# The first gate and up blocks of two FFNs: seven products in place of two whole blocks, in an order of their own

## The chip, the cores and the metric

The kernel runs on one core of a Trainium2 chip. The metric is the device time of one execution in microseconds (us), as the median of several runs. One execution was also recorded by the hardware profiler; all times of instructions are from that record. The engines are TensorE (PE), VectorE (DVE), ScalarE (ACT), GpSimd (POOL) and SyncE (SP), each with a queue of its own that it works off in order; DMAs are issued from SP and POOL.

## The reference, cut to what matters

Two layers over 512 tokens of width 1024: latent attention with an FFN, then chunked attention with an FFN. The change lies in both FFNs:

```python
def rms_norm(x, g):
    xf = x.astype(jnp.float32)
    y = xf * lax.rsqrt(jnp.mean(xf * xf, axis=-1, keepdims=True) + EPS)
    return (y * g.astype(jnp.float32)).astype(x.dtype)

def swiglu(h, w_gate, w_up, w_down):
    return (jax.nn.silu(h @ w_gate) * (h @ w_up)) @ w_down
```

Here h is the normed x (512 x 1024), and w_gate and w_up are 1024 x 2816, which is 22 column blocks of 128. All is float32.

## The kernel before, in words

Each float32 operand is split into two parts of the PE's fp32r type: ACT casts the value (`whi`, `th`, `xh`), DVE subtracts the cast from the value (`wlo`, `tl`, `xl`). One product of 128 rows of weights is then three matmuls (high by high, high by low, low by high). A weight tile of 1024 columns so costs one cast of ACT (L144) and one difference of DVE (L145); its data come by DMA into `raw`.

The FFN works on x before its norm's factor is known. Gate and up of blocks 0 and 1 are computed in four PSUM banks, the tokens in two halves, since the first half of x is ready earlier (`half`). Blocks 2 and 3 are computed next, whole, 96 matmuls of 128x512 in all (`proj`). In the meantime the sum of squares is transposed (`tot`), the factor is computed (`rstd`) and spread over partitions (`bc`), and the blocks are gated: gate times factor, silu, times up.

The 18 other blocks run as nine pairs. A pair's two blocks times the two halves of the width and the two halves of the tokens make a 2 x 2 by 2 x 2 block product, done by seven products instead of eight (`products`): 168 matmuls of 128x256 per pair, 24 per product. Weight sums (`sums`, `plus`) feed four of the seven; sums of blocks of x (`blocks_of`: the tiles `xg`, `t1`, `t3`, split into `th` and `tl`) are the moving operands. Products 1, 3, 4 and 5 accumulate in one pair of PSUM banks (`al`), product 2 has its own (`ga`), and products 0 and 6 share a third (`be`). Since each stands as a running sum that several results need, ACT or DVE take a copy out of a bank in between: of `be` after product 0 (`ut`), of `al` after products 1, 3 and 5 (`gt`, `gt`, `ut`). After product 6 the pair is gated.

The first pair's weight sums were made by DVE, from tiles that SP loads; from the second pair on, two of the sums come by DMAs on POOL's queue that add to what lies in the tile (`begin`), and DVE makes the two others. Down then runs over the gated blocks.

The order on each engine is set by a scheduler from the order of the code and priorities; `issue_after` (in the code also `behind`) makes one instruction stand after another. Weight tiles are split two ahead of the product that uses them (`feed.next(1024, 2)`).

## Time and profile before

| | |
|---|---|
| runs | 1103.98, 1104.80, 1104.91 us; median 1104.8 |
| profiled execution | 1105.07 us; its span, first to last instruction, 1103.3 us |
| mean granted PE clock | 0.997 |
| PE busy | 1092.4 us, 99% of the span, 6893 matmuls |
| DVE busy | 908.5 us, 82% |
| ACT busy | 678.3 us, 61% |
| POOL busy | 117.1 us, 11% |
| layer 0: blocks 2 and 3 / first pair begin | 212.07 us / 234.8 us |
| layer 1: the same | 787.20 us / 809.9 us |

Times within the span count from its first instruction. A row of the timeline has start, duration, engine, line, operation and the names of output and inputs, then in brackets the idle time ahead of it and what ended that. A duration runs until the result is there; where two instructions follow at once, the second starts a little before the first one's duration is over, so the cost of one in a queue is the difference of the starts. A line of the waits has the waiting engine and tile, the releasing engine and tile, then the sum, count and longest in us. The chain of waits names, for each stretch of time, the instruction that what comes later depended on.

### The profile page before, as it was taken

The page shows a single profiled execution, that of the slowest core. Times are in us where ns is not written, and L with a number is a line of the kernel's source. Part 1 is how long each engine was busy: PE and PEld are TensorE (multiplying, and loading weights), DVE is VectorE, ACT ScalarE, POOL GpSimd, SP SyncE. Part 2 cuts the span into 40 slices and gives each one's busy share as a digit, 9 for nine tenths or more (in the row PEclk, how much of TensorE's full clock was granted, in tenths as well). Part 3 has the DMA queues.
Part 4 walks back from the last instruction along what each step waited for, and adds up shares of the span by engine and source line. Part 5 has one row for each costly group of instructions (what it writes and reads, how often), then busy time and mean ns, then how long its engine had stood idle before and what let it go on. Part 6 is the DMA issues. An engine that isn't in the chain of part 4 may idle for free.

```text
span 1103.3 us, 19079 instructions
## 1 busy us (share of the span) xinstructions
PE 1092.4 (99%) x6893; PEld 978.8 (89%) x6893; DVE 908.5 (82%) x1659; ACT 678.3 (61%) x1323; POOL 117.1 (11%) x181
## 2 busy tenths in 40 slices
PE   9999999999999999999999999999999999999997
PEld 6887889999999998888888888889899999998885
DVE  7787747988878889978858898758988889789977
ACT  7575737655555556668636767657645555556675
POOL 2211100101000001500000110000100010001401
PEclk9999999999999999999999999999999999999999
DMA  7344226447787757961555677634638888758913
GB/s 240 120 116 142 62 68 238 143 116 184 171 202 184 180 167 248 164 191 49 190 153 156 173 192 186 168 121 161 198 103 214 228 207 223 216 178 249 171 29 76
DMA packets 88334, 181.47 MB, mean 164 GB/s; under 512 B 26816, under 2 KB 28608, under 8 KB 88240
## 3 DMA queue, kind: packets, MB, share of 16 engines
q1 hardware_dynamic: 74752, 147.10, 43.1%
q0 software_dynamic: 13056, 32.73, 16.4%
q8 instruction: 54, 0.88, 0.3%
q10 hardware_dynamic: 432, 0.44, 0.1%
q14 instruction: 40, 0.33, 0.1%
HBM read 148.88 MB, written 10.88 MB: 145 GB/s over the span
## 4 chain that ended last, share of the span: by engine, by line
PE 97%; DVE 1%; ACT 1%; issue 1%; DMA 0%; POOL 0%; DVEq 0%; POOLq 0%; SPq 0%; ACTq 0%
PE al L1550 19%; PE b L377 11%; PE b L378 11%; PE b L379 11%; PE be L1550 9%; PE al L1306 8%; PE be L1306 5%; PE ga L1550 5%; PE de L1306 3%; PE ga L1306 3%; PE pt L561 2%; PE b L1707 2%; PE b L1107 1%; PE sc L1699 1%; PE sc L1698 1%
## 5 line engine op out<-in xcount | busy, mean ns | idle before, releaser
L144 ACT CAST whi<-raw 128x1024 fp32r<-128x1024 f32 (+3 forms) x220 | 221.0, 1006 | 205.6 <-PE al L1550 71.5
L145 DVE TENSOR_TENSOR wlo<-raw,whi 128x1024 fp32r<-128x1024 f32 (+3 forms) x220 | 255.8, 1164 | 67.1 <-ACT whi L144 66.1
L1550 PE MATMUL al<-th,whi 128*128 128x256 f32 x432 | 122.8, 284 | 0.0
L1550 PE MATMUL al<-th,wlo 128*128 128x256 f32 x432 | 121.0, 280 | 0.0
L1550 PE MATMUL al<-tl,whi 128*128 128x256 f32 x432 | 121.0, 280 | 0.0
L377 PE MATMUL b<-xh,whi 128*128 128x512 f32 x234 | 96.7, 415 | 0.0
L378 PE MATMUL b<-xl,whi 128*128 128x512 f32 x234 | 91.8, 392 | 0.0
L379 PE MATMUL b<-xh,wlo 128*128 128x512 f32 x234 | 91.7, 392 | 0.0
L1550 PEld LDWEIGHTS al<-th,whi 128*128 128x128 f32 x432 | 81.3, 188 | 2.2
L1550 PEld LDWEIGHTS al<-th,wlo 128*128 128x128 f32 x432 | 81.3, 188 | 0.2 <-DVE wlo L145 0.2
L1550 PEld LDWEIGHTS al<-tl,whi 128*128 128x128 f32 x432 | 81.3, 188 | 0.0
L548 ACT ACTIVATE p<-p,mn 128x128 f32<-128x128 f32 (+1 forms) x96 | 54.1, 563 | 36.0 <-DVE mn L546 34.1
L145 DVE TENSOR_TENSOR ptl<-pt,pth 128x128 fp32r<-128x128 f32 (+1 forms) x96 | 46.6, 485 | 30.5 <-ACT pth L144 29.6
L145 DVE TENSOR_TENSOR wlo<-wd,whi 128x512 fp32r<-128x512 f32 x86 | 56.3, 684 | 14.6 <-ACT whi L144 14.4
L144 ACT CAST whi<-wd 128x512 fp32r<-128x512 f32 x86 | 49.8, 618 | 25.0 <-PE al L1306 10.7
L144 ACT CAST pth<-pt 128x128 fp32r<-128x128 f32 (+1 forms) x96 | 40.3, 422 | 32.2 <-PE pt L561 31.3
L171 POOL DMA_DIRECT2D raw<-in_w_pair x32 | 28.1, 895 | 285.9 <-DVE ut L1562 84.1
L379 PEld LDWEIGHTS b<-xh,wlo 128*128 128x128 f32 x234 | 43.9, 188 | 9.9 <-DVE wlo L145 0.3
L1306 PE MATMUL al<-whi,pl 128*128 128x512 f32 x132 | 51.5, 390 | 0.0
L1306 PE MATMUL al<-wlo,ph 128*128 128x512 f32 x132 | 51.4, 389 | 0.0
L1306 PE MATMUL al<-whi,ph 128*128 128x512 f32 x132 | 51.4, 389 | 0.0
L377 PEld LDWEIGHTS b<-xh,whi 128*128 128x128 f32 x234 | 44.2, 189 | 5.7 <-ACT whi L144 0.2
(320 smaller groups left out, 3391.2 us busy)
## 6 DMA issues: line engine op xcount, KB each, us to landing
raw<-in_w_pair SPq DMA_DIRECT2D x88, 512.0 KB, 4.6
raw<-in_w_pair POOLq DMA_DIRECT2D x32, 512.0 KB, 7.6
wd<-in_w_down SPq DMA_DIRECT2D x54, 256.0 KB, 6.0
raw<-in_w_o SPq DMA_DIRECT2D x16, 512.0 KB, 4.0
raw<-in_w_gu SPq DMA_DIRECT2D x16, 512.0 KB, 4.7
raw<-in_w_down SPq DMA_DIRECT2D x16, 512.0 KB, 4.3
raw<-in_w_qkb SPq DMA_DIRECT2D x16, 512.0 KB, 3.5
wd<-in_w_down POOLq DMA_DIRECT2D x22, 256.0 KB, 5.0
```

The source lines that it names most:

```text
L144: return (nc.scalar.copy(dst_hi, src), V.tensor_tensor(dst_lo, src, dst_hi.bitcast(F32), op=OP.subtract))
L145: V.tensor_tensor(dst_lo, src, dst_hi.bitcast(F32), op=OP.subtract))
L171: nc.gpsimd.dma_start(r[j], self.src[n], accum_op=OP.add)
L377: nc.tensor.matmul(o, l[0], r[0], start=start, stop=False)
L378: nc.tensor.matmul(o, l[0], r[1], start=False, stop=False)
L379: last_mm[0] = nc.tensor.matmul(o, l[1], r[0], start=False, stop=stop)
L548: nc.scalar.activation(p[:, :n], p[:, :n], AF.Exp, bias=mn[:, :1], scale=-1.0, accum_out=self.sums[:, qt:qt + 1])
L561: nc.tensor.transpose(t[:, kt * P:(kt + 1) * P], p[:, kt * P:(kt + 1) * P], ident)
L1107: nc.tensor.matmul(o[:, q_], va[kt][:, part, v_], pt[:, kt, q_], start=n + kt == 0, stop=n == 2 and kt == NQT - 1)
L1306: nc.tensor.matmul(to[e], l[c], r[d], start=j < 4 and k == 0 and n == 0, stop=k == NF // 2 - 1 and n == 2, skip_group_check=True)
L1550: nc.tensor.matmul(o, l[c], r[d], start=first_ and n == 0, stop=k == K2 - 1 and n == 2, skip_group_check=True)
L1707: nc.tensor.matmul(o[:, q_], vv, pt[:, kt, q_], start=pt is pth and kt == 0, stop=pt is ptl and kt == NQT - 1)
```

## The change

Blocks 2 and 3 leave the whole form (`N_WHOLE` from 4 to 2) and become a first pair, so that ten pairs run in place of nine. For that pair alone:

- Its seven products run in the order 1, 2, 0, 3, 6, 4, 5 (`FIRST_TURN`), and each product's matmuls are bound to stand after the one before.
- Its four weight sums come by DMAs on POOL's queue that add to a tile in SBUF: r0 is chunk 2 plus chunk 3, r3 is chunk 0 plus r0, r6 is chunk 1 plus r3, and r4 is chunk 2 plus chunk 0. The third waits for the second and the second for the first (`chain`); DVE makes none of them.
- The sums of blocks of x begin ahead of the second half of blocks 0 and 1; their later parts are laid between the differences of the weights of products 6, 4 and 5 (`step`).
- The fetch of x moves behind certain weight loads on SP's queue (`get_x`).
- ACT copies the four PSUM banks of blocks 0 and 1 to SBUF (`fu`). Squares, norm factor and its spreading move into the second and third pair, and the gating of blocks 0 and 1 and of the pairs becomes a list of units (`units`), taken one at a time within later pairs.
- In layer 1, a side job (`by_tokens`) starts in the third pair in place of the second.

The diff, cut to its core ("..." where lines are left out):

```diff
--- before.py
+++ after.py
-N_WHOLE = 4
+N_WHOLE = 2
...
+    FIRST_TURN = (1, 2, 0, 3, 6, 4, 5)
...
         def begin(self):
-            r, self.made = self.raw, True
-            r[0] = r[3] = r[6] = self.tile(2, wide[0], "sum", 2)
+            r = self.raw
+            r[0] = self.tile(2, wide[0], "sum", 2)
+            if self.turn[0]:
+                r[3] = self.tile(0, wide[0], "sum", 2)
+                r[6] = self.tile(1, wide[0], "sum2", 2)
+            else:
+                r[3] = r[6] = r[0]
             r[4] = self.tile(2, wide[0], "sum2", 2)
-            for j, n in ((0, 3), (4, 0)):
-                with tc.issue_after(last_pow[0].ins):
-                    nc.gpsimd.dma_start(r[j], self.src[n], accum_op=OP.add)
+            self.add(0, self.src[3])
+            self.add(4, self.src[0])
+
+        def add(self, j, src):
+            with tc.issue_after(last_pow[0].ins):
+                nc.gpsimd.dma_start(self.raw[j], src, accum_op=OP.add)
+
+        def chain(self):
+
+            self.add(3, self.raw[0])
+            self.add(6, self.raw[3])
...
         def sums(self, j):
...
-            if j == 0 and not self.made:
-                r[0] = r[3] = r[6] = wide[0].tile([P, 1024], F32, tag="sum", name=name_("raw"), bufs=2)
-                plus(r[0], r[4], r[5])
-            elif j in (3, 6):
+            if j in (3, 6) and not self.turn[0]:
                 plus(r[j], r[j], r[j // 3])
-            elif j == 4 and not self.made:
-                plus(r[4], r[4], r[1])
-            elif j == 1 and self.then:
+            if j == (3 if self.turn[0] else 1) and self.then:
                 self.then.begin()
...
-                for j in range(7):
-                    self.plan.append((pair, 1024, j, None))
+                if not p:
+                    pair.turn = FIRST_TURN
+                for j in pair.turn:
+                    self.plan.append((pair, 1024, j, None if p or j != 3 else "h"))
...
+            if not h:
+                with behind(feed.loaded):
+                    next(p for p, *_ in feed.plan[feed.pos:] if isinstance(p, Pair)).begin()
...
                 feed.ahead(2 if late else 3)
+                feed.loaded = get_x(feed.loads[feed.pos + (4 if late else 5)])
...
-        x = fetch(x_src)
+        x = []
         post = Post(G_APOST[i], H)
-        last = out_proj(osp, KT, post, firsts, 2, late)
+        last = out_proj(osp, KT, post, firsts, 2, late, lambda after: fetch(x_src, x, after))
...
-        sx.squares(0)
-        post.apply(x, 1, sx.each)
+        base = feed.pos
+        pair = feed.plan[base][0]
+        pair.chain()
+        feed.behind[base + 2] = feed.behind[base + 3] = post.apply(x, 1, sx.each)
+        tb, hid = [], Hidden(H)
+        more = blocks_of(x, G_FPRE[i], H, tb)
+        next(more)
+        feed.ahead(3)
         run(half(1))
-        sx.squares(1)
         for k in range(KT):
             nc.sync.dma_start(a["mid"][:, k], x[k])
-        tb = []
-        more = blocks_of(x, G_FPRE[i], H, tb)
-        next(more)
-        b = [bank(), bank()]
-        rest = proj(2, KT, 4, xs, b)
-        some(rest, 3)
-        v = sx.sum.total()
-        r = rstd(v)
+        kept = [H(name="fu") for _ in banks]
+        for t, b in zip(kept[:2], banks[:2]):
+            nc.scalar.copy(t, b)
+        with behind(next(more)[0]):
+            for t, b in zip(kept[2:], banks[2:]):
+                empty = nc.scalar.copy(t, b)
         eps = sp.tile([P, 4], F32, tag="eps", name=f"eps_{i}", bufs=1)
-        V.tensor_scalar(eps, v, EPS, None, op0=OP.mult)
-        some(rest, 7)
-        rb = spread_sb(r)
-        next(more)
-        banks.extend(b)
-        hid = Hidden(H)
-
-
-        for f in range(N_WHOLE):
-            if f < 3:
-                b = banks[2 * f:2 * f + 2]
-                if f == 2:
-                    run(rest)
-            else:
-                b = [bank(), bank()]
-                run(proj(2, KT, 4, xs, b))
-            t = U(name="gt")
-            V.tensor_tensor(t, b[0], rb, op=OP.mult)
+        rb = []
+
+        def norm():
+            v = sx.sum.total(None, 300)
+            with first(300):
+                r = rstd(v)
+            V.tensor_scalar(eps, v, EPS, None, op0=OP.mult)
+            rb.append(r)
+
+        def spread_():
+            rb[0] = spread_sb(rb[0])
+
+        def gate(t, u):
+            V.tensor_tensor(t, t, rb[0], op=OP.mult)
             nc.scalar.activation(t, t, AF.Silu)
             h = hid.room()
-            V.scalar_tensor_tensor(h, t, -1.0, b[1], op0=OP.mult, op1=OP.mult)
+            V.scalar_tensor_tensor(h, t, -1.0, u, op0=OP.mult, op1=OP.mult)
             hid.add(h)
-            if f == 1:
-                next(more)
-        products(xs, tb, rb, hid, by_tokens(H) if i else None)
+
+        low = []
+
+        def step(n):
+            low[:] = next(more)[1:] if not low else low
+            feed.lows[base + n] = low[0]
+            feed.split(base + n)
+            with behind(feed.low):
+                low[:] = next(more)[1:]
+            feed.lows[base + 6] = low[0]
+
+        side = {(0, 2): lambda: step(4), (0, 0): lambda: step(5), (1, 1): lambda: sx.squares(0),
+                (1, 4): lambda: sx.squares(1), (1, 6): norm, (2, 2): spread_}
+        units = [lambda f=f: gate(*kept[2 * f:2 * f + 2]) for f in range(N_WHOLE)]
+        products(xs, tb, rb, hid, side, units, empty, low, by_tokens(H) if i else None)
...
-        yield
+            last = split(*cut(out[k][0], A1), m[:, A1])
+        yield last
         for k in K2:
             u, v, m, n = ts[k]
             V.tensor_tensor(n[:, A0], v[:, A1], u[:, A1], op=OP.subtract)
             V.scalar_tensor_tensor(n[:, A1], m[:, A1], -1.0, v[:, A0], op0=OP.mult, op1=OP.subtract)
-            split(*out[k][1], n)
-        yield
+            last = split(*out[k][1], n)
+            if k:
+                yield last
...
-    def products(xs, tb, rb, hid, aside=None):
+    def products(xs, tb, rb, hid, side, units, empty, low, aside=None):
...
+        def gated(t, u):
+            V.tensor_tensor(t, t, rb[0], op=OP.mult)
+            nc.scalar.activation(t, t, AF.Silu)
+            h = hid.room()
+            V.tensor_tensor(h, t, u, op=OP.mult)
+            hid.add(h)
+
         pairs = (NF - N_WHOLE) // 2
+        done = mm = None
         for p in range(pairs):
             al, ga = [], []
             be = [bank("t" if p % 2 else "s", "be") for _ in range(2)]
-            gate = [U(name="gt") for _ in range(2)]
-            up_ = [U(name="ut") for _ in range(2)]
-            for j in range(7):
-                if aside is not None and p and j in (0, 1, 3, 5):
+            make = U if p > 3 else hid.make
+            gate = [make(name="gt") for _ in range(2)]
+            up_ = [make(name="ut") for _ in range(2)]
+            for j in (range(7) if p else FIRST_TURN):
+                if (p, j) in side:
+                    side[p, j]()
+                if p > 1 and j in ((3, 5) if p == 2 else (1, 3, 5)) and units:
+                    units.pop(0)()
+                if aside is not None and p > 1 and j in (0, 2, 4, 5, 6):
                     next(aside, None)
                 w = feed.next(1024, 2)
+                done = None if p else mm
                 if p + 1 == pairs and j >= 4:
                     hid.ahead(j // 5)
                 if j == 1:
@@ -1546,16 +1587,22 @@
                     for k in range(K2):
                         l, r = w(e * S + k * P, P), moving[j][k]
                         first_ = j < 3 and k == 0
-                        for n, (c, d) in enumerate(((0, 0), (0, 1), (1, 0))):
-                            nc.tensor.matmul(o, l[c], r[d], start=first_ and n == 0, stop=k == K2 - 1 and n == 2,
-                                             skip_group_check=True)
+                        with behind(done):
+                            for n, (c, d) in enumerate(((0, 0), (0, 1), (1, 0))):
+                                mm = nc.tensor.matmul(o, l[c], r[d], start=first_ and n == 0, stop=k == K2 - 1 and n == 2,
+                                                      skip_group_check=True)
                     t, u = gate[e], up_[e]
                     if j == 0:
                         nc.scalar.copy(u[:, A1], o)
+                        if not p:
+                            with behind(low[0]):
+                                V.tensor_tensor(t[:, A0], t[:, A0], ga[e][:, A0], op=OP.add)
                     elif j == 1:
-                        nc.scalar.copy(t[:, A0], o)
+                        with behind(None if p else empty):
+                            nc.scalar.copy(t[:, A0], o)
                     elif j == 2:
-                        V.tensor_tensor(t[:, A0], t[:, A0], o, op=OP.add)
+                        if p:
+                            V.tensor_tensor(t[:, A0], t[:, A0], o, op=OP.add)
                     elif j == 3:
                         nc.scalar.copy(t[:, A1], o)
                     elif j == 4:
@@ -1564,11 +1611,10 @@
                         nc.scalar.copy(u[:, A0], o)
                     else:
                         V.tensor_tensor(t[:, A1], t[:, A1], o, op=OP.add)
-                        V.tensor_tensor(t, t, rb, op=OP.mult)
-                        nc.scalar.activation(t, t, AF.Silu)
-                        h = hid.room()
-                        V.tensor_tensor(h, t, u, op=OP.mult)
-                        hid.add(h)
+                        units.append(lambda t=t, u=u: gated(t, u))
+                        while p > 6 and units:
+                            units.pop(0)()
```

How this moves instructions. On ACT, around the copies of product 0 in the first pair. Before (`be_635` is product 0's bank, `gt_618`, `gt_624`, `gt_633` belong to the gating of whole blocks, `th_585` is the last sum of x):

```order
L144 CAST th_581_2616<-t3_598_2641 128x512
L144 CAST th_585_2620<-t3_602_2649 128x512
L144 CAST whi_645_2874<-raw_611_2697 128x1024
L1200 ACTIVATE gt_624_2784<-gt_624_2784 128x512
L1554 COPY ut_639_2862<-be_635_2858 128x256
L1200 ACTIVATE gt_633_2849<-gt_633_2849 128x512
L144 CAST whi_648_2907<-raw_630_2819 128x1024
L1554 COPY ut_640_2863<-be_636_2859 128x256
L1556 COPY gt_637_2860<-al_650_2911 128x256
```

After (`be_604` and `be_605` are the banks of products 0 and 6, `al_610` and `al_611` those of 1, 3, 4 and 5; `whi_618` holds the weights of product 4, `whi_620` those of product 5, `whi_622` those of the next pair; `gt_606` L1602 copies product 1, L1607 product 3):

```order
L1198 COPY fu_602_2641<-b_530_2259 128x512
L1198 COPY fu_603_2642<-b_531_2260 128x512
L1602 COPY gt_606_2666<-al_610_2670 128x256
L1602 COPY gt_607_2667<-al_611_2671 128x256
L144 CAST whi_618_2744<-raw_522_2171 128x1024
L144 CAST th_559_2465<-t3_576_2482 128x512
L144 CAST th_563_2469<-t3_580_2490 128x512
L144 CAST whi_620_2806<-raw_492_2083 128x1024
L1607 COPY gt_606_2666<-al_610_2670 128x256
L144 CAST th_567_2473<-t3_584_2498 128x512
L1607 COPY gt_607_2667<-al_611_2671 128x256
L144 CAST th_571_2477<-t3_588_2506 128x512
L1596 COPY ut_608_2668<-be_604_2664 128x256
```

Before, the copy of product 0 stood ahead of product 1's copies; now it stands behind those of products 1 and 3 and behind the last four casts of the sums of x.

On DVE, the sums of x and the weight differences that those casts alternate with, after the change (`raw_521` is r6, so `wlo_614` belongs to product 6; `raw_522` is r4):

```order
L146 TENSOR_TENSOR tl_560_2466<-t3_576_2482,th_559_2465 128x512
L146 TENSOR_TENSOR tl_564_2470<-t3_580_2490,th_563_2469 128x512
L146 TENSOR_TENSOR wlo_614_2709<-raw_521_2169,whi_613_2708 128x1024
L1364 TENSOR_TENSOR t3_584_2498<-xg_582_2496,xg_581_2495 128x256
L1365 SCALAR_TENSOR_TENSOR t3_584_2498<-t1_583_2497,xg_582_2496 128x256
L146 TENSOR_TENSOR tl_568_2474<-t3_584_2498,th_567_2473 128x512
L146 TENSOR_TENSOR wlo_619_2745<-raw_522_2171,whi_618_2744 128x1024
L1364 TENSOR_TENSOR t3_588_2506<-xg_586_2504,xg_585_2503 128x256
L1365 SCALAR_TENSOR_TENSOR t3_588_2506<-t1_587_2505,xg_586_2504 128x256
```

Before, these sums and their differences stood between the splits of whole blocks, behind the squares and ahead of the gating; now each waits in turn for a cast on ACT and has a weight difference between it and the next.

On POOL, the DMAs of the first pair's weight sums (layer 0, after the change):

```order
L182 DMA raw_519_2165<-in_w_pair 128x1024
L496 TENSOR_TENSOR r_552_2349<-ss_551_2347,mhalf_92 128x2
L182 DMA raw_520_2167<-raw_519_2165 128x1024
L182 DMA raw_522_2171<-in_w_pair 128x1024
L182 DMA raw_521_2169<-raw_520_2167 128x1024
L182 DMA raw_594_2521<-in_w_pair 128x1024
```

The four DMAs on `raw_519` to `raw_522` are new; `r_552`, a factor of the norm behind attention, and the last DMA, which begins the next pair's sums, were there before.

More of the change, by code (lines that the diff above doesn't have):

```diff
@@ L140, in first, with split @@
         tc.cur_priority += n
-    def split(dst_hi, dst_lo, src):
-        return (nc.scalar.copy(dst_hi, src),
-                V.tensor_tensor(dst_lo, src, dst_hi.bitcast(F32), op=OP.subtract))
+    def split(dst_hi, dst_lo, src, after=None):
+        hi = nc.scalar.copy(dst_hi, src)
+        with behind(after):
+            return hi, V.tensor_tensor(dst_lo, src, dst_hi.bitcast(F32), op=OP.subtract)
     def split_scaled(dst_hi, dst_lo, src, col):
@@ L296, in load @@
                 if isinstance(src, Pair):
-                    src.load(j)
+                    self.loads[len(self.raw)] = src.load(j)
                     self.raw.append(None)
@@ L676, in apply, with fetch, out_proj @@
                         (nc.gpsimd if k in (0, 2, 4) else V).tensor_tensor(to(k), x[k][:, c], t, op=self.op)
-                    each(k, h)
-    def fetch(src, make=U):
-        x = []
-        for k in range(KT):
-            t = make(name="x")
-            nc.sync.dma_start(t, src[:, k])
-            x.append(t)
-        return x
-    def out_proj(rhs, n_k, post, have, n_last, late):
+                    at = each(k, h)
+            return at
+    def fetch(src, x, after=None):
+        with behind(after):
+            for k in range(KT):
+                t = U(name="x")
+                ins = nc.sync.dma_start(t, src[:, k])
+                x.append(t)
+        return ins
+    def out_proj(rhs, n_k, post, have, n_last, late, get_x):
         done = list(have)
@@ L1319, in blocks_of @@
         for k in range(KT // 2):
-            out.append([(U(F32R, "th"), U(F32R, "tl")) for _ in range(2)])
+            out.append([tuple(m(F32R, n) for n in ("th", "tl")) for m in (U, make if k == 3 else U)])
         K2 = range(KT // 2)
```

21 lines of the change are left out of this document (8 added, 13 removed).

## The prediction

> **What bounds the kernel now.** I read the page's busy times first, then TensorE's waits, then the chain of waits.
>
> ```profile
> PE 1092.4 (99%) x6893; PEld 978.8 (89%) x6893; DVE 908.5 (82%) x1659; ACT 678.3 (61%) x1323; POOL 117.1 (11%) x181
> PE 97%; DVE 1%; ACT 1%; issue 1%; DMA 0%; POOL 0%; DVEq 0%; POOLq 0%; SPq 0%; ACTq 0%
> PE sc L1094 <- ACT kh L144: 1.9, 1, 1.9
> PE warm L113 <- DVE idle L110: 1.2, 1, 1.2
> PE b L377 <- ACT xh L148: 0.2, 1, 0.2
> ```
>
> TensorE (PE) works 1092.4 of 1103.3 us and waits three times in all: 1.9 us in the first attention, 1.2 us at the start, 0.2 us in the second FFN. The chain is 97% PE. Time is thus gained by taking matmuls away and lost by making PE wait; what DVE or ACT do matters only where PE stands behind them. The next view is busy time by stretch. In each layer the first stretch runs from block 2's first matmul to the first pair's, the second over the first pair as far as its sixth product.
>
> ```profile
> 212.07:234.82 22.75, 22.75 (x107) 18.80 (x106) 20.60 (x43) 13.74 (x23) 2.90 (x3) 1.00 0.39 93
> 234.82:254.69 19.87, 19.87 (x169) 19.74 (x168) 16.52 (x24) 10.99 (x17) 0.86 (x1) 1.00 0.58 159
> 787.20:809.92 22.72, 22.72 (x106) 18.80 (x105) 20.09 (x43) 13.78 (x24) 3.22 (x3) 1.00 0.31 70
> 809.92:829.80 19.88, 19.88 (x168) 19.71 (x167) 17.67 (x24) 11.15 (x17) 0.83 (x1) 1.00 0.50 148
> ```
>
> After the window and its length stand PE, PEld, DVE, ACT, POOL (busy us, count), the clock granted to PE, the DMA share and GB/s. PE is full in all four, DVE is at 83% to 91%: beside PE there is little room on DVE.
>
> **The change part by part.** *Two blocks become a pair.* The chain gives the pieces.
>
> ```profile
> 214.30 0.44 PE tot L473 x4
> 219.55 0.44 PE bc L501 x4
> 237.80 2.82 PE al L1550 x24
> 257.70 2.82 PE al L1550 x24
> ```
>
> The two blocks take 22.75 us, in which 0.44 + 0.44 are transposes of the norm that stay. From one pair's second product to the next pair's is 257.70 - 237.80 = 19.90 us, seven products of 2.82 us. So a layer saves 22.75 - 0.88 - 19.90 = 1.97 us of PE, and both layers **3.9 us**, if PE gets through the new pair without waiting.
>
> *It does not, by the order.* The new pair's products run 1, 2, 0, 3, 6, 4, 5. Products 0 and 6 use the same two PSUM banks (`be`), so ACT must copy product 0 out (L1596, `ut_608`) before product 6 begins. Before, products 1 to 5 lay between them, 14.1 us; now only product 3 does, 2.82 us. In ACT's order that copy stands behind `gt_607`, which reads the second half of product 3 itself, and behind the cast `th_571`. `th_571` needs `t3_588`, which stands on DVE behind two 1024-column weight differences and two 512-column ones. For durations I use rows of the same operations in the trace of before (start to start where the next follows at once).
>
> ```profile
> 207.04 1.32 ACT L1325 ACTIVATE xg<-x,gains 128x512 f32<-128x512 f32 x2
> 217.17 1.00 ACT L144 CAST th<-t 128x256 fp32r<-128x256 f32 x3
> 220.02 0.59 ACT L508 COPY bc<-bc 128x512 f32<-128x512 f32 x1
> 229.39 1.05 ACT L144 CAST whi<-raw 128x1024 fp32r<-128x1024 f32 x1 [0.79 <-PE b L378]
> 230.35 1.66 ACT L144 CAST th<-t 128x512 fp32r<-128x512 f32 x3
> 236.43 0.37 ACT L1554 COPY ut<-be 128x256 f32<-128x256 f32 x1
> 236.69 0.64 ACT L1200 ACTIVATE gt<-gt 128x512 f32<-128x512 f32 x1
> 229.81 0.41 DVE L1338 TENSOR_TENSOR t<-xg,xg 128x256 f32<-128x256 f32 x1
> 230.15 0.41 DVE L1339 SCALAR_TENSOR_TENSOR t<-t,xg 128x256 f32<-128x256 f32 x1
> 230.99 0.69 DVE L145 TENSOR_TENSOR tl<-t,th 128x512 fp32r<-128x512 f32 x1 [0.44 <-ACT th L144]
> 231.60 1.22 DVE L145 TENSOR_TENSOR wlo<-raw,whi 128x1024 fp32r<-128x1024 f32 x1
> 232.74 0.68 DVE L145 TENSOR_TENSOR tl<-t,th 128x512 fp32r<-128x512 f32 x1
> ```
>
> ACT: 0.96 for a 1024-column cast (229.39 to 230.35), 0.52 to 0.55 for a 512-column one (1.66 for three), 0.30 for a 256-column one (1.00 for three, less the tail of the last), 0.62 for `xg` (1.32 for two), 0.48 for a 512-column copy (0.59 less its tail), 0.27 for a 256-column copy (236.43 to 236.69). DVE: 0.34 for 256 columns, 0.60 for 512, 1.14 for 1024 (231.60 to 232.74).
>
> I wrote the two orders out with these durations, each instruction starting when its engine is free and its inputs are done, from the same point of layer 0 as the trace (197 us). With the order of before this puts the start of Down within 0.5 us of the trace. With the new one: product 1 starts on PE at 212.0 (22.75 us of blocks no longer ahead of it), 2 at 214.8, 0 at 217.7, 3 at 220.5, and 6 is due at 223.4. ACT is at `fu_600` at 211.5 and has 8.1 us of work without a gap: two `fu` copies, four `xg`, four 256-column casts, `whi_613`, two `fu`, two `gt` copies, `whi_618` (0.96 + 2.5 + 1.2 + 0.96 + 0.96 + 0.54 + 0.96). So `th_559` starts at 219.5 and is done at 220.2. Then DVE: `tl_560`, `tl_564`, `wlo_614` and `t3_584` (0.60 + 0.60 + 1.14 + 0.75) until 223.3; ACT casts `th_567` until 223.9; DVE `tl_568`, `wlo_619` and `t3_588` (0.60 + 1.14 + 0.76) until 226.45; ACT casts `th_571` to 227.0 and copies `ut_608` to 227.36. Product 6 starts at 227.4: **PE stands 4.0 us**. Layer 1 has the same rows in the same order, and the ledger gives 4.0 again: **8.0 us** for both.
>
> The ends of this term: from below, `gt_607` cannot start before product 3 ends (223.4 + 0.2 for the last matmul to drain), and `gt_607`, `th_571`, `ut_608` (0.27 + 0.52 + 0.37) follow in one queue, so at least 1.4 us per layer even if DVE were never late. From above, 5 us, if each of the four hand-overs between ACT and DVE takes 0.2 us more. I take 4.0, since only a DVE 2.6 us ahead of the ledger would bring the lower end, and DVE is at 83% to 91% of its time here. Behind `ut_608` on ACT stand `ut_609` and `whi_622`, the next pair's first weights; these wait for the buffer that product 6 gives back, so they move with PE and cost nothing more. On DVE the additions of product 6's banks move with it too.
>
> *What the wait does to PE's clock.* The one long wait of PE in before is followed by this:
>
> ```profile
> 106.67 0.50 PE L1094 MATMUL sc<-kh,qh 128*128 128x128 f32 x2 [1.92 <-ACT kh L144]
> 100.00:104.00 4.00, 4.00 (x22) 3.23 (x21) 3.42 (x10) 3.44 (x10) 0.00 (x0) 1.00 0.47 109
> 104.00:108.00 4.00, 2.08 (x13) 1.57 (x11) 3.38 (x6) 3.60 (x7) 1.28 (x2) 0.94 0.61 152
> 108.00:112.00 4.00, 4.00 (x20) 3.90 (x19) 3.24 (x9) 1.72 (x5) 0.52 (x1) 0.63 0.67 253
> ```
>
> After 1.92 us without matmuls the granted clock falls: 4 x (0.06 + 0.37) = 1.72 us of PE work lost. A stall of 4.0 us is twice as long, and I expect the same after each. Some of the slow stretch can fall inside the stall, where it costs nothing; I take 1.45 of 1.72, with 0.75 and 1.72 as ends, so **2.9 us** for both layers. Waits under 1 us I do not charge with it. [...]
>
> *Other waits.* The gatings of blocks 0 and 1 and of the first two pairs are put off into later pairs, where DVE has 2.2 us of room (17.67 of 19.88).
>
> ```profile
> L1567 DVE TENSOR_TENSOR gt<-gt,bc 128x512 f32<-128x512 f32 x36 | 24.9, 692 | 1.2
> L1570 DVE TENSOR_TENSOR hd<-gt,ut 128x512 f32<-128x512 f32 x36 | 23.1, 683 | 0.0
> ```
>
> One gating more per pair is 0.69 + 0.68 plus about one 256-column sum (0.42), so about 1.8 us, and the room is nearly used up. The ledger finds PE behind DVE or ACT by 0.05 to 0.47 us at two further places in layer 0 (0.4 us in all) and six in layer 1 (1.1): **1.5 us**; ends 0 and 3. The 0.2 us wait of before at `xh` in layer 1 goes, as a third weight difference (1.14) no longer stands ahead of the values it needs on DVE: **-0.2**; next behind it is `xh` of the following tile, 0.6 us early.
>
> *Work that I cost at nothing.* The first pair's sums leave DVE for DMAs that accumulate, each waiting for the one before.
>
> ```profile
> raw<-in_w_pair SPq DMA_DIRECT2D x88, 512.0 KB, 4.6
> raw<-in_w_pair POOLq DMA_DIRECT2D x32, 512.0 KB, 7.6
> ```
>
> With the first base loaded at 186, three links of 7.6 us land at 194, 202 and 209; the last, r6, is read by `whi_613` at 215.8, so 6 us to spare; r4 lands in between. Should the links take 10 us each, the last would come at 216 and begin to push `whi_613`. The x loads go behind weight loads on SP; in the ledger the first is issued near 177 and needed at 184, and the weight loads, larger ones, take 4.6 us. The four `fu` copies (0.48 each) and seven casts instead of four (3 x 0.96) are on ACT, whose busy share in the first stretch is 13.74 of 22.75; they are inside the ledger. DVE loses four 1024-column sums and gains three differences. Binding product to product adds no wait, since PE runs its queue in order.
>
> **The sum.** -3.9 + 8.0 + 2.9 + 1.5 - 0.2 = +8.3 us. The profiled execution took 1105.07 us, 0.3 above the median of the runs, 1104.8; put on the median, **1113.1 us**, with 1111 to 1116 as this case's own range (clock term 1.5 to 3.4, other waits 0.5 to 3).
>
> **The rivals.**
> - *The stall without the slow clock.* PE stands 4.0 us twice, but the clock stays at 1.00: 1104.8 - 3.9 + 8.0 + 1.5 - 0.2 = 1110.2. For it: that the one observed fall came after a wait among short, scattered matmuls, whereas here PE is dense before and after. Against it: the wait here is twice as long.
> - *DVE runs ahead, and the copies come early.* If DVE has `t3_588` ready by 223.9, ACT's order alone decides, 1.4 us in each layer, and the clock stays: -3.9 + 2.8 + 1.5 - 0.2 = +0.2, **1105.0**; without the other waits 1103.5, and only if PE also needed not wait for `gt_607` would the full saving show, 1101. It decides from the point where DVE gains 2.6 us between 211 and 224, for which ACT would have to give `th_559` before 217.5. For it: ACT has 39% idle time in the whole. Against it: the 8.1 us without a gap ahead of `th_559`.
> - *Half of it.* DVE gains about 1.7 us, and PE stands 2.3 us twice, too spread for the clock: -3.9 + 4.6 + 1.3 = +2.0, 1106.8.
> - *The chain of DMAs is late.* Links of 11 us (3.4 more each, 10 in all) would bring r6 4 us after 215.8, the stall to 8 us in each layer, 1121; half of that, 1117. Against it: 7.6 is the median of 32 such loads.
> - *The change does not do what it says*, if the products were not run in the bound order: the built order shows them bound, so I give it nothing of its own.
>
> **How the numbers follow.** Forecast 0.50; stall without the clock 0.22; half 0.10; early copies 0.12; late chain 0.06. Least change that can be told from none: 0.2%, 2.2 us. Slower by more than that (above 1107.0) are the forecast, the second case, the late chain and two fifths of the half case: 0.82. Same takes the rest of the half case and half of the early copies: 0.12. Faster, below 1102.6, needs the early copies without `gt_607`'s wait or the other waits, 0.06. The range is 1105.6 to 1116.5: it leaves out the early copies and most of the late chain, some 0.16.
>
> **What would show it.** Right: on PE an idle of about 4 us just before product 6 of the first pair of each layer, put down to ACT's copy of `ut` (L1596); on ACT, `th` just ahead of it waiting for DVE; a granted clock below 1.00 in the 4 us behind it; nothing put down to DMA between 180 and 235 us. Wrong: an idle of 1.4 us or less there, with `ut` copied by 225 us; or idle before product 1 or 2, which would mean the chain of DMAs or the `fu` copies.

## The result, and the profile after

The changed kernel takes 1118.15 us (median of 4 runs, 1116.68 to 1120.31) against 1104.39 us before (median of 4). The ratio is 1.0127, 95% interval 1.0106 to 1.0149: slower by 13.8 us, where 8.3 were forecast, and above the range's end of 1116.5. The profiled execution took 1119.37 us, with a span of 1117.6.

The page's busy times, after:

```profile
PE 1095.1 (98%) x7037; PEld 987.6 (88%) x7037; DVE 914.6 (82%) x1675; ACT 691.5 (62%) x1355; POOL 129.1 (12%) x193
```

The waits of TensorE, after:

```profile
PE be L1592 <- ACT ut L1596: 7.5, 2, 3.8
PE sc L1109 <- ACT kh L144: 1.9, 1, 1.9
PE al L1592 <- DVE ut L1609: 1.8, 2, 1.6
PE be L1592 <- ACT fu L1198: 0.8, 2, 0.6
PE al L1592 <- ACT gt L1607: 0.6, 2, 0.4
PE be L1592 <- DVE wlo L146: 0.3, 1, 0.3
```

The first wait is the predicted one, twice 3.75 us: product 6 of the first pair of each layer for ACT's copy of product 0. Its chain in layer 0 is seen in the timelines of ACT and DVE (the last row is PE's):

```profile
221.74 1.05 ACT L144 CAST whi<-raw 128x1024 fp32r<-128x1024 f32 x1
223.24 0.37 ACT L1607 COPY gt<-al 128x256 f32<-128x256 f32 x1 [0.45 <-PE al L1592]
224.26 0.62 ACT L144 CAST th<-t 128x512 fp32r<-128x512 f32 x1 [0.65 <-DVE t L1365]
224.78 0.37 ACT L1607 COPY gt<-al 128x256 f32<-128x256 f32 x1
227.44 0.62 ACT L144 CAST th<-t 128x512 fp32r<-128x512 f32 x1 [2.29 <-DVE t L1365]
227.96 0.64 ACT L1596 COPY ut<-be 128x256 f32<-128x256 f32 x2
224.91 0.69 DVE L146 TENSOR_TENSOR tl<-t,th 128x512 fp32r<-128x512 f32 x1 [0.69 <-ACT th L144]
225.52 1.22 DVE L146 TENSOR_TENSOR wlo<-raw,whi 128x1024 fp32r<-128x1024 f32 x1
226.65 0.42 DVE L1364 TENSOR_TENSOR t<-xg,xg 128x256 f32<-128x256 f32 x1
226.99 0.42 DVE L1365 SCALAR_TENSOR_TENSOR t<-t,xg 128x256 f32<-128x256 f32 x1
228.38 0.58 PE L1592 MATMUL be<-xh,whi 128*128 128x256 f32 x1 [3.75 <-ACT ut L1596]
```

The copy (`ut<-be`) needs nothing but product 0, done since about 221.8. It stands idle behind a cast that waits 2.29 us for DVE. Product 6 was forecast at 227.4 in a run whose first product began at 212.0; here that is 212.6, and 228.4.

Busy time by stretch, from the first pair or block to Down in layer 0, and from the norm's last transposes to Down in layer 1. Before:

```profile
212.07:414.49 202.42, 202.42 (x1618) 197.30 (x1617) 170.65 (x253) 113.27 (x180) 15.18 (x17) 1.00 0.66 170
771.49:989.79 218.30, 218.06 (x1743) 212.56 (x1742) 191.41 (x302) 122.58 (x203) 15.25 (x17) 1.00 0.71 196
```

After, with the clock behind the two stalls:

```profile
212.61:421.52 208.91, 204.31 (x1690) 202.56 (x1689) 175.61 (x266) 121.62 (x205) 17.67 (x19) 0.98 0.69 176
778.61:1003.90 225.29, 218.60 (x1815) 216.31 (x1814) 194.14 (x309) 131.50 (x225) 20.14 (x22) 0.99 0.78 203
224.00:228.00 4.00, 0.64 (x6) 0.43 (x4) 2.72 (x5) 1.45 (x4) 0.00 (x0) 0.88 0.82 223
228.00:232.00 4.00, 3.62 (x17) 3.62 (x18) 2.91 (x5) 0.60 (x3) 1.74 (x2) 0.50 0.91 204
232.00:236.00 4.00, 4.00 (x28) 4.00 (x28) 1.61 (x3) 1.05 (x1) 0.00 (x0) 0.76 1.02 215
810.00:814.00 4.00, 4.00 (x24) 4.00 (x24) 2.28 (x5) 0.00 (x0) 1.71 (x2) 0.59 0.77 179
814.00:818.00 4.00, 4.00 (x35) 4.00 (x34) 3.08 (x5) 1.93 (x2) 0.00 (x0) 0.98 0.97 223
```

The two stretches grow by 6.5 and 7.0 us; the other 0.8 of the 14.3 us between the spans lie outside these stretches. PE's idle time in them goes from 0.24 to 11.29 us: 7.5 us more in the stalls, 3.6 more in other waits. PE's busy time grows by 2.43 us though, by the count of its matmuls, it has 3.94 us less to do. At half rate it loses 4 x (0.12 + 0.50 + 0.24) = 3.4 us in layer 0, of which about 0.7 fall inside the stall (half rate from 228 - 0.48 / 0.5 = 227.0 on, product 6 from 228.4), and 4 x (0.41 + 0.02) = 1.7 in layer 1, so 4.46 in all. The remaining 1.9 us (2.43 + 3.94 - 4.46) are longer steps between matmuls at a few places per pair, too short to be listed as waits; their causes were not separated.

### The profile page after: what moved, and what is told of

Read it like the earlier page. It is cut to its first block, busy times and chain, and to the rows that moved or that the text cites. A ratio compares the mean times of both kernels' runs of the same rounds, so it can differ in the third digit from the quotient of the medians.

```text
span 1117.6 us, 19433 instructions
## 1 busy us (share of the span) xinstructions
PE 1095.1 (98%) x7037; PEld 987.6 (88%) x7037; DVE 914.6 (82%) x1675; ACT 691.5 (62%) x1355; POOL 129.1 (12%) x193
## 5 line engine op out<-in xcount | busy, mean ns | idle before, releaser
L1592 PE MATMUL al<-th,whi 128*128 128x256 f32 x464 | 132.5, 285 | 2.6 <-DVE ut L1609 1.8
L1592 PE MATMUL al<-tl,whi 128*128 128x256 f32 x464 | 130.0, 280 | 0.0
L1592 PE MATMUL al<-th,wlo 128*128 128x256 f32 x464 | 130.0, 280 | 0.0
L1592 PEld LDWEIGHTS al<-th,whi 128*128 128x128 f32 x464 | 87.5, 189 | 5.7 <-DVE ut L1609 3.0
L390 PE MATMUL b<-xh,whi 128*128 128x512 f32 x170 | 71.8, 422 | 0.0
L182 POOL DMA_DIRECT2D raw<-in_w_pair x40 | 35.7, 906 | 270.9 <-DVE wlo L146 93.7
L392 PE MATMUL b<-xh,wlo 128*128 128x512 f32 x170 | 66.9, 393 | 0.0
L391 PE MATMUL b<-xl,whi 128*128 128x512 f32 x170 | 66.9, 393 | 0.0
L1592 PE MATMUL be<-xh,whi 128*128 128x256 f32 x160 | 46.8, 293 | 7.5 <-ACT ut L1596 7.5
L1592 PE MATMUL be<-xh,wlo 128*128 128x256 f32 x160 | 46.8, 292 | 0.3 <-DVE wlo L146 0.3
```

Of the source, the lines that this page charges most:

```text
L182: nc.gpsimd.dma_start(self.raw[j], src, accum_op=OP.add)
L390: nc.tensor.matmul(o, l[0], r[0], start=start, stop=False)
L391: nc.tensor.matmul(o, l[0], r[1], start=False, stop=False)
L392: last_mm[0] = nc.tensor.matmul(o, l[1], r[0], start=False, stop=stop)
L1592: mm = nc.tensor.matmul(o, l[c], r[d], start=first_ and n == 0, stop=k == K2 - 1 and n == 2, skip_group_check=True)
```

## The experiments

The verdicts go by ratios to the kernel before, run on the same chip in between. Where two of the kernels are compared with each other, their times come from different sets of runs, so the difference of their distances to their own runs of before is given too.

### The copy ahead of the last sum of x

```diff
-        side = {(0, 2): lambda: step(4), (0, 0): lambda: step(5),
+        side = {(0, 2): lambda: step(4), (0, 3): lambda: step(5, out0[0]),
...
-            with behind(feed.low):
+            with behind(extra), behind(feed.low):
                 low[:] = next(more)[1:]
```

(`out0[0]` holds the second copy of product 0, `extra` the argument of `step`.)

> Changed kernel, with the last sum of x (t3 and th of k = 3) put behind ACT's copies of product 0, so that the copies stand right after the first copy of product 3; nothing else is moved by hand. My theory (product 6 waits for the copy, and the copy for its place in ACT's queue): the stalls of 3.75 us before product 6 go to 0.5 us or less in both layers, the half-rate clock in the FFNs goes with them (4.5 us in the profile of the changed kernel), and about 0.9 us of new waits per layer appear at product 4 and at the next pair's product 1; together 1118.2 - 7.0 - 4.5 + 1.8 = 1108.5, between 1106.5 and 1110.5. Rival (the sums themselves are late, whatever the place of the copy): the wait moves to product 4 at its full size, 3 us or more in each layer, and the time stays above 1115.

Measured 1107.93 us (7 runs), ratio 1.0027 (1.0015 to 1.0039). ACT's timeline:

```profile
222.27 0.37 ACT L1607 COPY gt<-al 128x256 f32<-128x256 f32 x1 [0.44 <-PE al L1592]
222.54 0.66 ACT L1596 COPY ut<-be 128x256 f32<-128x256 f32 x2
223.29 0.62 ACT L144 CAST th<-t 128x512 fp32r<-128x512 f32 x1
```

The copies are done at 223.2 in place of 228.6, PE does not wait before product 6, and the clock stays at full rate in both FFNs (mean over the profiled run 0.997, as before; 0.993 in the changed kernel). The cast of the last sum runs at 227.41, as late as in the changed kernel (227.44), and now nothing long stands behind it. What comes instead is a wait of 0.59 us per layer for a cast of the next pair's weights. One place in a queue is worth 10.2 of the 13.8 us (10.5 by the distances to before); the time lies in the range of the first theory, and the rival, sums that make PE wait wherever the copy stands, falls.

### PE kept busy in the stall

```diff
+                if not p and j == 6:
+                    dummy = bank("t", "dummy")
+                    for n in range(28):
+                        with behind(done):
+                            done = nc.tensor.matmul(dummy[:, A0], xs[0][0][:, :P], xs[1][0][:, A0], start=True, stop=True)
```

> Changed kernel, with 28 matmuls of 128x256 on operands at hand, into a bank that nobody reads, in the first pair of each layer between products 3 and 6: 28 x 0.117 = 3.3 us of work in the 3.75 us in which PE waits. If the half-rate clock comes from PE's idleness, no half-rate stretch is left in the FFNs and the time falls by what it cost, 2.8 us in layer 0 and 1.7 in layer 1 in the profile: 1118.2 - 4.5 = 1113.7, between 1112 and 1115.5, with product 6 starting as late as before. Rival (the clock falls for another reason, such as the load of the FFN): the half-rate stretches stay and the time stays at 1117 to 1120.

Measured 1118.59 us (4 runs), ratio 1.0129 (1.0111 to 1.0147): no gain. But the theory's own sign was there. Busy time by stretch, around the stall of layer 0 and then later in layer 1:

```profile
224.00:228.00 4.00, 3.61 (x30) 3.40 (x29) 3.31 (x6) 1.40 (x4) 0.00 (x0) 1.00 0.89 265
228.00:232.00 4.00, 4.00 (x36) 4.00 (x36) 2.82 (x6) 1.05 (x1) 1.73 (x2) 1.00 0.60 119
856.00:864.00 8.00, 6.02 (x51) 5.82 (x49) 2.28 (x5) 2.74 (x4) 0.00 (x0) 1.00 0.91 224
872.00:880.00 8.00, 5.44 (x33) 5.24 (x33) 7.31 (x10) 2.05 (x3) 0.86 (x1) 0.79 0.99 251
```

DVE's largest wait in the same kernel between 840 and 920 us:

```profile
DVE xt L1248 <- DMA x<-mid: 5.7, 1, 5.7
```

The clock is 1.00 behind the stall, in both layers. But the side job's transpose stood 5.7 us on DVE for its load, PE then waited 2.4 and 2.6 us, and the clock fell there. The run mixed two causes and by its time alone decided nothing.

### The side job in its places of before

```diff
-                if aside is not None and p > 1 and j in (0, 2, 4, 5, 6):
+                if aside is not None and p and j in (0, 1, 3, 5):
```

> Changed kernel, with layer 1's side job (by_tokens: loads of mid, transposes on DVE) back in its four places per pair from the second pair on. In the changed kernel DVE waits 1.7 us for such a load at 907 us and PE 1.6 us at 918. If the job's place is the cause, that wait goes and the time falls by about 1.5 us to 1116.7, between 1115 and 1118; if DVE's deferred gatings are the cause, a wait of the same size appears in another of the pairs 2 to 6 and the time stays within 0.7 us of 1118.2. The clock's falls may blur this by a microsecond or two, so the waits in the trace decide.

Measured 1115.95 us (4 runs), ratio 1.0098 (1.0083 to 1.0113): 2.2 us faster than the changed kernel (2.4 by the distances to before), as expected. DVE no longer waits for `x<-mid`, and PE's wait for `ut` (L1609) is gone. The rows of the changed kernel that it removes, DVE and PE:

```profile
909.10 0.71 DVE L1248 STREAM_TRANSPOSE xt<-x 128x512 f32<-128x512 f32 x1 [1.68 <-DMA x<-mid]
918.37 0.39 PE L1592 MATMUL al<-th,whi 128*128 128x256 f32 x1 [1.57 <-DVE ut L1609]
```

The chain of waits in the changed kernel leads from PE's wait at 918.37 back over DVE to the load of `x`, 7.61 us from 901.46 on. Not all of the gain need be this: in the two profiled executions the half rate in layer 0 also lasted 3.41 us here in place of 6.83, and this edit does not touch layer 0.

### Product 6 last

```diff
-    FIRST_TURN = (1, 2, 0, 3, 6, 4, 5)
+    FIRST_TURN = (1, 2, 0, 3, 4, 5, 6)
```

> Changed kernel with the first pair's products in the order 1, 2, 0, 3, 4, 5, 6, so that three products lie between 0 and 6. My theory (DVE and ACT make the late sums of x too late, the copy was only the first place where PE met them): the wait before product 6 goes, but product 4 waits in its middle for the last sum of x, and the next pair's first product for its weights; about 3.2 us in all in each layer in place of 3.75, in two parts, the longer some 1.5 to 2.5 us; 1113 to 1118. Rival (having only one product between 0 and 6 is the whole cause): no wait above 0.5 us in the first pair, 1107 to 1109.

Measured 1116.86 us (4 runs), ratio 1.0107 (1.0092 to 1.0122). The waits of PE:

```profile
PE al L1592 <- DVE ut L1609: 3.1, 2, 1.7
PE al L1592 <- ACT th L144: 2.5, 2, 1.2
PE be L1592 <- ACT whi L144: 2.1, 2, 1.1
PE al L1592 <- DVE tl L146: 0.4, 2, 0.2
```

No product waits for the copy now, and yet 2.5 us per layer are left in the first pair (1.23 + 0.21 + 1.06, the last three rows; 3.2 were forecast), in the middle of product 4 for the last sum of x and behind the pair for weights. The sums are late as well; the first experiment, with product 6 ahead of them and its copy free, hides that. The first row is the side job in layer 1 again, 3.1 us in place of the changed kernel's 1.8, and the clock fell once more in layer 1 (mean over the profiled run 0.995), so the time tells little and the waits decide.

### The copy first, and the side job as before

The edits of the first and the third experiment together.

> The kernel with the copy first (1107.9) and, in addition, layer 1's side job in its four places of before. My theory (two separate faults: the copy's place, and the side job's transposes on DVE that wait for their loads): the gains add, 1107.9 - 2.2 = 1105.7, between 1104.5 and 1106.8, and no PE wait above 0.7 us is left in the FFNs. Rival (the first fault hid the second, or DVE is simply full): the time stays at 1107 or above, with a wait of over 1 us for DVE in layer 1.

Measured 1105.5 us (10 runs), ratio 1.0014 (1.0004 to 1.0023). The gains add: 10.2 and 2.2 alone, 12.7 together (10.5, 2.4 and 12.4 by the distances to before). No wait of PE above 0.6 us is left in the FFNs. The two are separate faults.

### PE kept busy, and the side job as before

The edits of the second and the third experiment together.

> The kernel with 28 spare matmuls in the stall, and the side job in its places of before, so that the waits of layer 1 do not lower the clock either. To be compared with the kernel with the side job alone, 1115.95, which has one half-rate stretch of 3.41 us in each layer. If the clock costs what its stretches say, both go and the time falls by 2 x (0.75 to 1.7) us, to 1113.3, between 1112.3 and 1114.6; product 6 starts as late as before. If half rate costs nothing there (because DVE and ACT catch up while PE is slow, and waits shrink by as much): 1115 to 1117.

Measured 1112.98 us (4 runs), ratio 1.0079 (1.0064 to 1.0095), and 1.00 of clock in every stretch behind the stalls. Against 1115.95 with the stall idle that is 3.0 us, 2.5 by the distances to before: so two half-rate stretches cost 2 to 3 us here, and the two intervals leave more room than that. Product 6 begins as late as with the side job alone (in layer 0 at 227.6 us, there at 227.9), so the idleness itself, and not the waiting, lowers the clock here.

### Without the binding

```diff
-                done = None if p else mm
+                done = None
```

> Changed kernel without the binding of the first pair's products to each other; the scheduler then lays half of product 4 ahead of product 6. My theory (PE waits in its own order for late sums; work that is ready stands behind the waiting product): the stall is split and shrinks from 3.75 to about 2.3 us per layer (0.6 before the second half of product 4, 1.4 in it, 0.3 at product 5), and no idle stretch is long enough for the clock to fall: 1118.2 - 2 x 1.7 - 4.5 = 1110.3, between 1108.5 and 1113. Rival (the binding is harmless, since PE had nothing else that was ready): 1116.5 to 1119.

Measured 1109.49 us (4 runs), ratio 1.0058 (1.0039 to 1.0076): 8.7 us faster than the changed kernel, in the range of the theory. PE's largest waits in the FFNs:

```profile
PE al L1592 <- DVE wlo L146: 2.2, 2, 1.1
PE al L1592 <- DVE ut L1609: 1.8, 4, 0.8
PE al L1592 <- ACT gt L1607: 1.3, 4, 0.4
```

The stall of 3.75 us is broken into waits of at most 1.1 us, and the clock in the FFNs stays up (mean over the profiled run 0.998). In layer 0 part of product 4 now runs from 222.4 to 226.6 us, ahead of product 6. With the products bound, product 4 could not use the time in which product 6 waited.

### The copies of blocks 0 and 1 on DVE

To the kernel with the copy first and the side job as before:

```diff
         for t, b in zip(kept[:2], banks[:2]):
-            nc.scalar.copy(t, b)
+            V.tensor_copy(t, b)
...
             for t, b in zip(kept[2:], banks[2:]):
-                empty = nc.scalar.copy(t, b)
+                empty = V.tensor_copy(t, b)
```

> The kernel with the copy first and the side job as before, and the four copies of blocks 0 and 1 (fu) on DVE in place of ACT, where ACT has 8.1 us of work without a gap and DVE waits for it. If ACT is what makes the sums of x late, the waits at the copies (0.24 in layer 0, 0.3 to 0.9 in layer 1) go: 0.3 to 1 us faster than with the copies on ACT, 1104.9, between 1104.0 and 1106; that would still be no change against before (1104.6). Rival (the copies only change places, and DVE's 0.6 us each delay the sums themselves): 1106 to 1108.

Measured 1104.74 us (11 runs) against 1104.17 before, ratio 1.0008 (1.0000 to 1.0017): the changed kernel's loss is gone, but nothing is won. PE no longer waits for `fu`; the 0.8 us against the kernel with the copies on ACT (1105.5) lie within the two intervals.

### Room of its own for product 5's weights

```diff
-                    self.plan.append((pair, 1024, j, None if p or j != 3 else "h"))
+                    self.plan.append((pair, 1024, j, None if p or j not in (3,5) else "h"))
```

> The kernel with the copy first, the side job as before and the fu copies on DVE, with one further edit: the weights of product 5 of the first pair get a room of their own in the pool of 512-column tiles (as product 3's have), so that the split tiles of the next pair no longer wait for products 6 and 4 to give theirs back. In the kernel without it, PE waits 0.59 us in each layer for the cast of such a tile (at 229.3 and 803.7 us). If the missing buffer is the cause, both waits go, 1104.74 - 1.2 = 1103.5, between 1102.7 and 1104.5, at or slightly below before (1104.2). Rival (ACT and DVE are too late there with or without a buffer): a wait of the same size moves to the next product, 1104.5 to 1105.5.

Measured 1107.44 us (6 runs), ratio 1.0036 (1.0023 to 1.0049): a miss, 2.7 us slower than without. ACT's timeline in layer 1:

```profile
798.30 1.04 ACT L144 CAST whi<-raw 128x1024 fp32r<-128x1024 f32 x1 [3.87 <-DMA raw<-in_w_pair]
799.25 0.37 ACT L1607 COPY gt<-al 128x256 f32<-128x256 f32 x1
799.51 0.65 ACT L1596 COPY ut<-be 128x256 f32<-128x256 f32 x2
```

With a free buffer the next pair's cast moved up in ACT's queue, to a place ahead of the copies of product 0, and waited there for its weight sum. PE waited 2.5 us for the copy: the changed kernel's fault again, with a DMA in DVE's part.

### That cast behind the copies

```diff
-(0, 3): lambda: step(5, out0[0]),
+(0, 3): lambda: (feed.behind.update({base + 7: (out0[0],)}), step(5, out0[0])),
```

> The kernel with a room of its own for product 5's weights (1107.4), in which ACT stood 3.9 us in layer 1 for the next pair's first weight sum, a DMA of POOL's queue that landed at 798.3, with the first copy of product 3 and the copies of product 0 behind it and PE 2.5 us behind these. One edit: the cast of that sum is put behind the copies of product 0. If the place in ACT's queue was the cause once more, the waits of 0.57 and 2.51 us before product 6 go, and nothing above 0.4 us is left in the first pair: 1107.4 - 3.1 - 0.8 = 1103.5, between 1102.8 and 1104.6, against before at 1104.0: faster by 0 to 0.1%. Rival (the sum itself is late for what needs it): PE waits 1 us or more at product 4 or at the next pair's first product, and the time stays at 1105 or above.

Measured 1105.64 us (11 runs) against 1105.14, ratio 1.0007 (0.9997 to 1.0018). The waits before product 6 are gone, but PE waits 1.38 us at 803.2 in layer 1 for the difference of that sum's weights. In layer 0 the stretch to Down takes 202.1 us in place of 202.4, in layer 1 the sum itself is late: the rival held there, and in the time too. No kernel tried beats before.

## Why the prediction was right and wrong

- **What bounds the kernel, and the saving.** Right that PE bounds the kernel and its waits decide. The 3.9 us are right by the count of matmuls, but no run shows them whole: with the copies on DVE, where the clock stays at full rate in the FFNs (mean over the profiled run 0.999), PE is busy for 201.18 us from the first pair to Down in layer 0, against 202.42 before, 1.2 less where 1.97 were forecast. What is missing can only lie in longer steps between matmuls, which the sum left out, and is part of why no kernel tried beats before.
- **The stall before product 6.** Right in place, chain and size: 8.0 forecast, 7.5 measured, and shown by moving the copy past the casts that waited. The lower end rested on `gt_607` ahead of the copy; with the copy moved past it the stall was nil. That binding the products adds no wait was wrong: unbound, part of product 4 filled the time, and the kernel gained 8.7 us.
- **The clock.** Right in kind, wrong in size: 2.9 forecast, 4.5 in the profile, 2 to 3 where two single stretches were removed. The step took one stretch per stall. In layer 0 the half rate went on for a second one: the rows from 224 to 236 us lose 3.4 us, twice the 1.7 of layer 1. The runs show that idleness decides (0.88, 0.50 and 0.76 in those rows, 1.00 in all three with PE kept busy). In layer 0 the clock fell at 227.07 us, 2.4 us into the stall, and in layer 1 PE was busy for 1.04 of the 3.41 us ahead of the fall.
- **Other waits.** Here the prediction failed. 1.5 us were forecast, less 0.2; the idle time beside the stalls grew by 3.6, with 1.9 more in steps too short to be listed: 5.5 in place of 1.3. Of the 6.0 us by which the profile exceeds the sum, this is 4.2, the clock 1.6, the time outside the two stretches 0.8, and the stalls give 0.5 back. The largest of the waits is one the sum had no term for, 1.8 us: the side job in layer 1, moved to five places per pair. By the code, four of its eight transposes so stand one product behind their load, 2.8 us, where two did before, and the load takes 5.6 in the median. It was in the diff, and not followed. Its place is worth about 2 us, and in the run with PE kept busy, where DVE stood 5.7 us for a load, PE lost 5.0 us to waits there. What makes the longer steps stays open.
- **The range.** The ends of the clock (1.5 to 3.4) and the other waits (0.5 to 3) give 1110.7 to 1115.1 and not 1111 to 1116; the stall's own upper end, 5 us per layer, was left out, and with it 1117 would have been the end.
- **Work costed at nothing.** The chain of DMAs was to be 6 us early; it was 0.3 late, as ACT's timeline shows:

```profile
216.75 1.05 ACT L144 CAST whi<-raw 128x1024 fp32r<-128x1024 f32 x1 [0.34 <-DMA raw<-raw]
```

  The DMA issues between 176 and 230 us (count, size, median us to landing), and the busy time by stretch, with the DMA share before the last column:

```profile
raw<-raw POOLq DMA_DIRECT2D x2, 512.0 KB, 8.4
```

```profile
186.00:191.00 5.00, 5.00 (x44) 5.00 (x43) 4.99 (x15) 3.38 (x9) 0.12 (x1) 1.00 1.00 376
191.00:196.00 5.00, 5.00 (x45) 5.00 (x44) 3.96 (x10) 2.93 (x5) 1.57 (x2) 1.00 1.05 354
```

  The links from tile to tile took 8.4 us in place of 7.6 and the first was issued at 190.9, some 5 us after the point that the sum took; the DMA engines were full from 186 to 196 us, where before they stood idle (shares of 0.01 and 0.00). The late-chain rival was closer than its 0.06 said, though ACT's wait for it was only 0.3 us in layer 0 and 0.4 in layer 1.
- **The rivals.** The stall without the slow clock is refuted. Early copies were not what happened; the first experiment made them by order, at 1107.9 where that rival had 1105.0.

## What to carry to other kernels

An instruction whose input has long been ready can still be late by its place in a queue (here the copy of product 0, 6.2 us behind the product's end): before an order is accepted, look at what stands ahead of each copy that frees a PSUM bank, and what that waits for; a cast that depends on another engine or on a DMA belongs behind it. Bind matmuls to an order only where nothing else could fill a wait (without the binding the kernel gained 8.7 us), and count a wait on TensorE with the half-rate stretch that may follow it (here 6.83 and 3.41 us at half rate, each at a wait of 3.75 us). When a side job moves, compare the distance between its load and its first use with the load's own time (here 2.8 us and 5.6), since the engine that uses it will stand still with everything behind it (DVE for 1.68 us in the changed kernel, for 5.7 us with PE kept busy).

## What the runs showed of the hardware

The same wait of 1.92 us in the first attention does not always lower the clock. Before and in the changed kernel it did (0.94 and 0.63, 0.95 and 0.62 in the two rows around it), in three of the later kernels not: the one without the binding and the two of the copies on DVE and of product 5's own room. The first two of these:

```profile
104.00:108.00 4.00, 2.07 (x12) 1.44 (x11) 3.34 (x7) 3.92 (x7) 0.94 (x2) 1.00 0.61 146
108.00:112.00 4.00, 4.00 (x27) 3.65 (x26) 3.86 (x10) 1.99 (x6) 0.86 (x2) 1.00 0.77 251
104.00:108.00 4.00, 2.08 (x14) 1.55 (x12) 3.38 (x6) 3.64 (x7) 0.96 (x2) 1.00 0.60 134
108.00:112.00 4.00, 4.00 (x27) 3.58 (x27) 3.86 (x10) 2.28 (x7) 0.84 (x2) 1.00 0.77 285
```

PE's idle time is the same to 0.01 us. What differs is where the wait falls. In the traces of before and of the changed kernel the changes of the granted clock lie whole multiples of 3.413 us apart: in the changed kernel it changes, among others, at 107.60, 227.07, 233.90 and 810.75 us, 35, 2 and 169 times that length from one to the next, and the falls between 100 and 1000 us last 3.41, 6.83 and 3.41 us. Here is the time in windows of that length, counted from such a change: those with the wait of 1.92 us before and in the kernel without the binding, then two of the stall in layer 0 of the changed kernel:

```profile
104.11:107.53 3.42, 1.50 (x9) 1.04 (x8) 2.89 (x4) 3.42 (x7) 0.83 (x2) 1.00 0.57 122
102.91:106.32 3.41, 2.16 (x14) 1.55 (x12) 2.21 (x7) 3.31 (x8) 0.75 (x1) 1.00 0.46 100
223.66:227.07 3.41, 0.97 (x9) 0.77 (x7) 2.73 (x6) 0.89 (x2) 0.00 (x0) 1.00 0.96 269
227.07:230.48 3.41, 2.10 (x10) 2.10 (x11) 2.73 (x5) 1.16 (x3) 0.86 (x1) 0.50 0.79 181
```

Before, one window held the whole wait, and the next ran at half rate. Without the binding (counted from the change at 3.92 us) the wait ran on past the window's end, 1.25 us of it fell into the window, and the clock stayed. Of the windows counted so between 100 and 1000 us, before and in the changed kernel, those at full rate with up to 1.57 us of idle PE were followed by full rate, and the four with 1.92 to 2.43 us by half rate; what lies between is not shown. A window that was itself at half rate was followed by half rate with 1.31 us idle (the last row), where 1.38 us at full rate, in layer 1 from 803.92 to 807.34, did no harm; that is one case alone.

In the 21 runs of before that go with the fifth to eighth experiments, the clock shows in the time: ten with a mean clock of 0.998 or more took 1103.15 to 1104.17 us, eleven with 0.997 or less 1104.02 to 1105.47. The changed kernel's runs spread over 3.6 us, but its mean clock does not order them (0.992 in the fastest, 0.993 in the slowest), so the cause of that spread is not shown.
